# Background scans in a decoder layer: smaller steps, four queues in turn, one operation fewer per chunk state

## The chip, the core and the metric

One Trainium2 chip, one core of it. The metric is the device time of one execution in microseconds (us), lower is better; the number given is the median of the runs shown. Engines: TensorE (PE), VectorE (DVE), ScalarE (ACT), GpSimd (POOL), and SyncE (SP), whose queue starts the transfers.

## What is computed

One inference step of a decoder layer for 1024 prompt tokens and 32 sample tokens (8 sequences of 4) that share the weights, width 1024. Three token mixers run on one input projection: GLA (4 heads, key width 64), FoX attention (4 heads of 128) and HGRN2 (4 heads of 128). Their gated sum goes through `w_out`, then come a SwiGLU block and a last RMSNorm. GLA and HGRN2 are the same gated linear scan:

```
b = cumsum(log_a, within a chunk)
A[t,s] = sum_k q[t,k] k[s,k] exp(b[t,k] - b[s,k])   for s <= t
o = A v + (q exp(b)) S
S = exp(b_last) S + (k exp(b_last - b))^T v
o_a = rms_norm(o_a) * g * silu(gate)
```

The outputs are the activations, the scans' last states for prompt and samples, and FoX's keys, values and forget logs.

## The kernel before

**Layout and products.** All 1056 tokens lie along the free dimension, features on 128 partitions. An fp32 product of full accuracy is made from three fast ones: weight and input are each split into a high and a low part (`split`, L214 and L215), and `gemm` (L115) issues high·high, high·low and low·high per block k of 128 features, in chunks of 352 tokens (L136). A job with 8 blocks has 3 chunks of 24 products; a branch job (4 blocks) 3 chunks of 12.

**Stages.** norm1 and the first jobs (to about 83 us); `in_pairs`, most of the input projection, in which one stage (`pair_run`, L1813) shares sums of operands between pairs of output blocks and FoX's attention runs beside (to 690 us); the mixer stage: 16 jobs for the branch gates and then the first branch jobs, with the scans in the background (690 to 1083 us); a check whether every scan stayed in its safe range (`any_range`, L1437, with a slow path behind a branch that these inputs don't take); the remaining branch jobs, `w_out`, the SwiGLU block and the last norm.

**The background.** Each scan is a Python generator that issues instructions up to its next `yield`. Three queues hold them: `bg3` with two `gla_pair` (L1041), `bg4` with four `hgrn_head` (L1062), and `bgs`, which a `scan` fills with a `scan_sample` (L1340). `gemm` takes one step of `bg3` and of `bgs` after block 3 of every chunk and one of `bg4` and `bgs` at the end of a chunk:

```
if k == 3 and job.kt == KD:
    self.pump(self.bg3, self.bgs)
...
self.pump(self.bg4, self.bgs, *(() if job.kt == KD else (self.bg3,)))
```

At the eighth branch job `second` (L1541) drains what is left.

A scan step is large. `scan` (L1093) makes the cumulated sums (`sums`, L1233), then for each half of 512 tokens `scan_pairs` (DVE subtract and clamp at L1154 and L1155, two exponentials on ACT, two products on POOL at L1158 and L1159), `scan_scores` (matmuls L1172 and L1173, masked copy L1176, transposes L1181), `scan_states` (matmuls L1193; then per chunk ACT L1204, DVE L1205, ACT L1206) and `scan_out` (L1219 and L1221). `scan_sample` prepares its operands (`pair_tile`, L1236 to L1249) one yield before the score matmuls at L1372; then come L1379, L1389, L1394, L1395 and, for the new states, L1413. `head_norm` (L1077, with `rstd` at L229) ends a scan: squares, sums over the partitions, a Newton refinement in three chunks, the gate, and a store to DRAM from where the branch jobs read it. The activations q, k and the decay hold their slots from the first step to the last.

**What sets the order.** The order in which Python issues is a priority only: a scheduler with its own estimates of durations places the instructions on each engine, so a step can stand earlier or later than it was issued. Each engine then works in order.

**ROLL.** In `pair_run` the weights of the next pair are split piece by piece between products, by a table from step to pieces (`ROLL`, L1764); S1 is a DVE subtract (L1753) that needs freshly loaded weights, P1 to P7 are splits.

Of the kernel before, what the change touches and what calls it, by code (L numbers as in the profile page):

```python
# [18 lines left out]
NP = 1024  # L19
# [18 lines left out]
NA, NBU, NH, NAT = 10, 8, 10, 4  # L38
# [52 lines left out]
class Body:  # L91
    def __init__(self, nc, tc, A, O):
        self.nc, self.tc, self.A, self.O = nc, tc, A, O
        self.bg, self.bgs, self.bg3, self.bg4 = [], [], [], []
# [20 lines left out]
    def gemm(self, job, nxt):  # L115
# [13 lines left out]
        for c in range(0 if job.tiles_first else NCW):  # L129
# [3 lines left out]
            for k in range(job.kt):  # L133
# [4 lines left out]
                if k == 3 and job.kt == KD:  # L138
                    self.pump(self.bg3, self.bgs)
# [4 lines left out]
            self.pump(self.bg4, self.bgs, *(() if job.kt == KD else (self.bg3,)))  # L144
# [43 lines left out]
    def pump(self, *qs):  # L188

        if self.cold:  # L190
            return
        for q in qs or (self.bg3, self.bgs, self.bg4):
            if q and next(q[0], "end") == "end":
                q.pop(0)

# [117 lines left out]
    def phase_m(self):  # L313
# [16 lines left out]
        self.bg3 += [self.gla_pair(p) for p in range(2)]  # L330
        self.bg4 += [self.hgrn_head(h) for h in range(4)]
# [323 lines left out]
    def hgrn_gate(self, h, z):  # L655
        nc = self.nc
        l, la = self.u.get(), self.u.get()
# [4 lines left out]
        nc.scalar.activation(z, z, AF.Exp, scale=-1.0, bias=self.log1mlb[:, h:h + 1])  # L662

        nc.vector.tensor_scalar(la, la, self.log1mlb[:, h:h + 1], None, ALU.add)
        nc.scalar.activation(l, la, AF.Abs, bias=self.nloglb[:, h:h + 1])
        nc.scalar.activation(l, l, AF.Exp, scale=-1.0)
        nc.scalar.activation(l, l, AF.Ln, bias=self.one1)
        nc.vector.scalar_tensor_tensor(la, la, self.loglb[:, h:h + 1], l, ALU.max, ALU.add)
        self.u.put(l)
        return z, la  # L670
# [23 lines left out]
    def gla_decay(self, p):  # L694
        nc = self.nc
        z, l = self.u.get(), self.u.get()
        for j in range(4):
# [4 lines left out]
            self.pm.put(ps)  # L702
        self.logsig_part(z, l)
        nc.vector.scalar_tensor_tensor(z, z, 0.0, l, ALU.min, ALU.subtract)
        nc.vector.tensor_scalar(z, z, 1.0 / 16.0, None, ALU.mult)
        self.u.put(l)
        return z
# [333 lines left out]
    def gla_pair(self, p):  # L1041
        yield from self.room(7)
        q, k, *vT = [self.fetch(*t) for t in (("gq", p), ("gk", p), ("gv", 2 * p), ("gv", 2 * p + 1))]
        la = self.gla_decay(p)
        yield
# [9 lines left out]
        yield from self.room(3)  # L1055
        os = [self.u.get(), self.u.get()]
        yield from self.scan(p, q, k, la, vs, vn, os, 64, self.A["sgla"][p], self.O["sgla_p"][p], self.O["sgla_s"][p])
        self.u.put(q, k, la, *vu)
        for i in range(2):
# [1168 lines left out]
```

## Time and profile before

| | us |
|---|---|
| median of the 3 runs | 2011.99 (2006.44 to 2013.47) |
| the profiled execution | 2009.41 |
| its span from the first to the last instruction | 2007.6 |
| PE busy in the span | 1938.9 (97%) |
| DVE busy | 1366.0 (68%) |
| ACT busy | 820.4 (41%) |
| POOL busy | 451.7 (22%) |

The mean granted clock of TensorE over the span is 0.979 of 2.4 GHz. Engines overlap, so the shares don't add up to 100%. Matmuls are pipelined: a row of the timeline gives when the first of a group started and how long the group took, and the next may start before that ends. "L136 <- DVE u" reads: the instruction of line 136 waited for DVE's write to u.

### The profile page before, as it was taken

The numbers are of one execution on the slowest core, as the hardware profiler recorded it, in microseconds if no ns is written. First come the engines' busy times: TensorE is split into PE (matmuls) and PEld (weight loads), VectorE is DVE, ScalarE is ACT, GpSimd is POOL, SyncE is SP. The second block draws the span as 40 slices with busy tenths as digits, with TensorE's granted clock in tenths as the row PEclk, the third lists the DMA queues.
The fourth block names the chain that finished last, engine by engine and source line by source line (L and its number), as shares of the span: only waits on it lengthen the run. The fifth ranks groups of instructions, "written<-read, shape, count | busy, mean of one in ns | idle before, by whom it ended". The sixth has DMA issues, their size and how long they took to land. (4 is left out here: it accounts for less than half of the span.)

```text
span 2007.6 us, 36645 instructions
## 1 busy us (share of the span) xinstructions
PE 1938.9 (97%) x14590; PEld 1821.8 (91%) x14590; DVE 1366.0 (68%) x2267; ACT 820.4 (41%) x1485; POOL 451.7 (22%) x271
## 2 busy tenths in 40 slices
PE   8999999999999999999999999999999999999997
PEld 6889999888988977778899999999999999999997
DVE  8866557544666576866653555878777887668965
ACT  5444444322433354544452343543333333323435
POOL 5211011211222121312100541123222322110004
PEclk9999999999999998979899999999999999999998
DMA  3443432577565533423543443121222122333212
GB/s 142 147 138 121 132 117 85 158 228 228 194 204 187 186 114 115 148 104 141 172 153 115 154 168 118 65 85 64 96 84 77 65 76 76 135 116 121 84 59 87
DMA packets 96982, 253.59 MB, mean 126 GB/s; under 512 B 14562, under 2 KB 28066, under 8 KB 96802
## 3 DMA queue, kind: packets, MB, share of 16 engines
q1 hardware_dynamic: 95250, 249.96, 36.5%
q8 instruction: 117, 1.92, 0.4%
q10 hardware_dynamic: 1296, 0.67, 0.1%
q14 instruction: 63, 0.52, 0.1%
q0 software_dynamic: 256, 0.52, 0.1%
HBM read 183.74 MB, written 67.37 MB: 125 GB/s over the span
## 5 line engine op out<-in xcount | busy, mean ns | idle before, releaser
L136 PE MATMUL pg<-x,wh 128*128 128x352 f32 x1692 | 425.8, 332 | 5.2 <-ACTq L1441 3.2
L1813 PE MATMUL pg<-x,wh 128*128 128x264 f32 x2080 | 401.5, 288 | 7.1 <-POOL frmul L754 2.6
L1813 PEld LDWEIGHTS pg<-x,wh 128*128 128x128 f32 x2080 | 322.8, 188 | 19.9 <-issue 9.6
L136 PEld LDWEIGHTS pg<-x,wh 128*128 128x128 f32 x1692 | 300.6, 192 | 13.3 <-issue 4.3
L1813 PE MATMUL pg<-x,wl 128*128 128x264 f32 x1040 | 295.6, 284 | 0.4 <-DVE wl L215 0.4
L136 PE MATMUL pg<-x,wl 128*128 128x352 f32 x846 | 278.4, 329 | 0.0
L1813 PEld LDWEIGHTS pg<-x,wl 128*128 128x128 f32 x1040 | 195.7, 188 | 0.6 <-DVE wl L215 0.6
L1813 PE MATMUL pg<-x,rh 128*128 128x264 f32 x976 | 187.6, 288 | 2.8 <-DVE fu L1820 2.8
L1813 PE MATMUL pg<-pr,wh 128*128 128x264 f32 x832 | 164.5, 294 | 0.1
L136 PEld LDWEIGHTS pg<-x,wl 128*128 128x128 f32 x846 | 162.7, 192 | 0.0
L1813 PEld LDWEIGHTS pg<-x,rh 128*128 128x128 f32 x976 | 152.2, 189 | 6.3 <-DVE fu L1820 3.2
L215 DVE TENSOR_TENSOR wl<-wf,wh 128x512 fp32r<-128x512 f32 (+2 forms) x125 | 109.7, 880 | 54.0 <-ACT wh L214 43.1
L214 ACT ACTIVATE wh<-wf 128x512 fp32r<-128x512 f32 (+2 forms) x125 | 77.5, 620 | 157.1 <-PE pg L1813 123.9
L1813 PE MATMUL pg<-x,rl 128*128 128x264 f32 x488 | 139.3, 285 | 0.0
L1813 PEld LDWEIGHTS pg<-pr,wh 128*128 128x128 f32 x832 | 130.0, 190 | 9.5 <-issue 5.6
L573 POOL TENSOR_TENSOR pu<-pu,r 128x1056 f32<-128x1056 f32 x21 | 57.3, 2731 | 321.2 <-ACT pu L1822 321.2
L1813 PE MATMUL pg<-pr,wl 128*128 128x264 f32 x416 | 119.0, 286 | 0.0
L1869 POOL TENSOR_TENSOR fu<-fu,r 128x1056 f32<-128x1056 f32 x22 | 67.3, 3059 | 216.9 <-ACT fu L1822 203.7
L107 ACT ACTIVATE wh<-wf 128x1024 fp32r<-128x1024 f32 (+2 forms) x60 | 51.3, 855 | 158.5 <-PE pg L136 143.6
L1820 DVE TENSOR_TENSOR pu<-pu,pg 128x264 f32<-128x264 f32 x132 | 55.8, 426 | 67.0 <-PE pg L1813 66.1
L1822 ACT ACTIVATE pu<-pg 128x264 f32<-128x264 f32 x176 | 66.6, 381 | 67.7 <-PE pg L1813 60.1
L1813 PEld LDWEIGHTS pg<-x,rl 128*128 128x128 f32 x488 | 92.3, 189 | 0.0
(521 smaller groups left out, 4409.6 us busy)
## 6 DMA issues: line engine op xcount, KB each, us to landing
z_dram<-pu SPq DMA_DIRECT2D x44, 528.0 KB
wf<-in_wgu SPq DMA_DIRECT2D x44, 512.0 KB
fa<-in_kc SPq DMA_DIRECT2D x64, 256.0 KB
fa<-in_vc SPq DMA_DIRECT2D x64, 256.0 KB
u<-z_dram SPq DMA_DIRECT2D x30, 528.0 KB
wf<-in_winp SPq DMA_DIRECT2D x30, 512.0 KB
ub<-z_dram SPq DMA_DIRECT2D x22, 528.0 KB
wf<-in_win SPq DMA_DIRECT2D x19, 512.0 KB
```

The costliest lines, as they stand in the source:

```text
L107: nc.scalar.activation(wh[:, :n], wf[:, :n], AF.Copy)
L136: nc.tensor.matmul(ps[:m, :CW], a[:, k, :], b[:, sl], start=n == 0, stop=n == 3 * job.kt - 1)
L214: nc.scalar.activation(h, x, AF.Copy)
L215: (eng or nc.vector).tensor_tensor(l, x, h.bitcast(F32), ALU.subtract)
L573: e[i].tensor_tensor(y[i], y[i], self.r1, ALU.mult)
L1813: nc.tensor.matmul(ps, a[:, w], b, start=first and m == 0, stop=m == 3 * K - 1, skip_group_check=not first)
L1820: nc.vector.tensor_tensor(out, out, ps, ALU.add)
L1822: nc.scalar.activation(out, ps, AF.Copy)
L1869: TT = lambda e, o, x, y, op=ALU.mult: e.tensor_tensor(o, x, y, op)
```

## The change

It has seven parts.

1. `gemm` calls a new `tick` after every block (three products) in place of the two pumps per chunk. `tick` takes one step of one queue; four queues take turns, empty ones are passed over. The fourth, `bgn`, holds the head norms. `hgrn_head(3)` moves from `bg4` to `bg3`.
2. The scans yield more often, and an operation that feeds a matmul is issued one or more yields before it: scores and outputs per head, transposes, states, gates, decay, sample steps, norm steps.
3. Operands are given back early: the samples' columns of q, k and b are copied to small tiles (POOL), so that q, k and the decay go back once both halves are multiplied. Output slots and the norm's gate are fetched late. There are 9 half-size slots instead of 10.
4. States: f2 = f0 of the chunk before times f1 of this one (POOL, once), then T·f2 + U is one DVE operation and T·f2, the scaled state for the outputs, one ACT operation.
5. From DVE to ACT: a bias in the HGRN gate, the 1/16 in the GLA decay, a copy per head in the sample scan.
6. The norm's refinement is done over the whole width instead of three chunks.
7. `ROLL`: S1 one step later, and other pieces moved with it.

```diff
-                if k == 3 and job.kt == KD:
-                    self.pump(self.bg3, self.bgs)
+                self.tick()
...
-            self.pump(self.bg4, self.bgs, *(() if job.kt == KD else (self.bg3,)))
...
+    def tick(self):
+        qs = self.bg3, self.bgs, self.bg4, self.bgn
+        for _ in () if self.cold else qs:
+            q = qs[self.turn % 4]
+            self.turn += 1
+            if q:
+                self.pump(q)
+                return
...
-        self.bg3 += [self.gla_pair(p) for p in range(2)]
-        self.bg4 += [self.hgrn_head(h) for h in range(4)]
+        self.bg3 += [self.gla_pair(0), self.gla_pair(1), self.hgrn_head(3)]
+        self.bg4 += [self.hgrn_head(h) for h in range(3)]
...
+        small = [sp.tile([128, NS], F32, tag="s" + m, name="s" + m, bufs=4) for m in "qkb"]
+        for t, x in zip(small, (q, k, b)):
+            nc.gpsimd.tensor_copy(t, x[:, NP:NT])
...
+        nc.gpsimd.tensor_tensor(f[:, 2, 1:8], f[:, 0, 0:7], f[:, 1, 1:8], ALU.mult)
+        yield
+        self.scan_mul(1, q, k, qe[1], ke[1])
+        self.u.put(q, k, la)
...
+            for h in range(len(vs)):
+                self.scan_scores(At[h], hs[h], qe[hf], ke[hf])
+                yield
...
+            for h in range(len(vs)):
+                self.scan_out(hf, qe[hf], At[h], Sm, vs[h], hs[h], os[h])
+                yield
...
-                nc.scalar.activation(Sm[:, cs], T, AF.Copy, scale=f[:, 0, g - 1:g])
-                nc.vector.scalar_tensor_tensor(Tt[:, cs], Sm[:, cs], f[:, 1, g:g + 1], U[:, cs], ALU.mult, ALU.add)
-                nc.scalar.activation(Sm[:, cs], Sm[:, cs], AF.Copy, scale=f[:, 1, g:g + 1])
+                nc.vector.scalar_tensor_tensor(Tt[:, cs], T, f[:, 2, g:g + 1], U[:, cs], ALU.mult, ALU.add)
+                before.append((Sm[:, cs], T, f[:, 2, g:g + 1]))
...
+        for o, t, g in before:
+            nc.scalar.activation(o, t, AF.Copy, scale=g)
...
+        for m in (2, 1):
+            nc.scalar.activation(E[m], E[m], AF.Exp)
+        nc.scalar.activation(eb, b, AF.Exp)
+        nc.scalar.activation(kh, kh, AF.Exp)
+        yield
...
-    ROLL = {3: (1, "P1", "S1"), 4: (1, "P5", "S2"), 5: (1, "P6", "S3"), 6: (1, "P2", "S4"), 0: (0, "P7"), 1: (0, "P3"), 2: (0, "P4")}
+    ROLL = {3: (1, "P1"), 4: (1, "S1"), 5: (1, "P5", "S2"), 6: (1, "P6", "S3"), 0: (0, "P2", "S4"), 1: (0, "P7", "P3"), 2: (0, "P4")}
```

**How the order moves.** On PE, about 216 products into the mixer stage, before: products (L136; x and wh, wl are the split input and weights), the sample scan's first score matmul (L1372, from skq) between two of them, then a scan half's transposes and scores (L1181, L1172, L1173).

```order
L136 MATMUL pg_96<-x_88,wh_71 128x352
L136 MATMUL pg_96<-x_87,wl_73 128x352
L136 MATMUL pg_96<-x_89,wh_71 128x352
L1372 MATMUL pg_97<-skq 32x32
L136 MATMUL pg_96<-x_90,wh_71 128x352
L1181 MATMUL pg_94<-c_ident,h_8127 128x128 x4
L136 MATMUL pg_96<-x_89,wl_73 128x352
L1172 MATMUL pg_93<-h_8126,h_8127 64x128
L1173 MATMUL pg_93<-h_8126,h_8127 64x64
L1172 MATMUL pg_93<-h_8126,h_8127 64x128
L1173 MATMUL pg_93<-h_8126,h_8127 64x64
```

On PE after, where the same sample scan's scores stand (now L1453; transposes of its keys are L1461, states L1264, prompt outputs L1291 and L1293, products L138):

```order
L138 MATMUL pg_96<-x_79,wh_71 128x352
L138 MATMUL pg_96<-x_80,wh_71 128x352
L138 MATMUL pg_96<-x_79,wl_73 128x352
L1453 MATMUL pg_97<-skq_8423 32x32
L1453 MATMUL pg_98<-skq_8427 32x32
L1453 MATMUL pg_92<-sq,sk 32x32
L1461 MATMUL pg_93<-c_ident,skh 32x128
L138 MATMUL pg_96<-x_81,wh_71 128x352
L138 MATMUL pg_96<-x_82,wh_71 128x352
L138 MATMUL pg_96<-x_81,wl_73 128x352
L1264 MATMUL pg_94<-ub_8145,h_8133 128x128 x4
L138 MATMUL pg_96<-x_83,wh_71 128x352
```

All sample scores of a head stand together, between two sets of three products, and no score of the prompt is beside them.

On PE before, the end of a run of 49 rows without a product: prompt outputs (L1219, L1221), new sample states (L1413), the norm's sums (L229), then products again.

```order
L1219 MATMUL pg_98<-at_8136,ub_8146 128x128
L1221 MATMUL pg_98<-h_8133,h_8132 128x128
L1219 MATMUL pg_98<-at_8136,ub_8146 128x128
L1221 MATMUL pg_98<-h_8133,h_8132 128x128
L1413 MATMUL pg_92<-h_8134,skt 64x512
L1413 MATMUL pg_93<-h_8128,skt 64x512
L1413 MATMUL pg_93<-h_8131,skt 64x512
L229 MATMUL pg_94<-u_8119,ones 128x352
L229 MATMUL pg_97<-u_8119,ones 128x352
L229 MATMUL pg_98<-u_8119,ones 128x352
L136 MATMUL pg_95<-x_85,wh_72 128x352
L136 MATMUL pg_95<-x_86,wh_72 128x352
```

On PE after, prompt outputs of the same stretch and the sample scan's past part (L1471):

```order
L1471 MATMUL pg_94<-u_8121,h_8130 32x128 x8
L138 MATMUL pg_95<-x_77,wh_72 128x352
L138 MATMUL pg_95<-x_78,wh_72 128x352
L138 MATMUL pg_95<-x_77,wl_74 128x352
L1291 MATMUL pg_97<-at_8135,ub_8145 128x128
L1293 MATMUL pg_97<-h_8132,h_8125 128x128
L1291 MATMUL pg_97<-at_8135,ub_8145 128x128
L1293 MATMUL pg_97<-h_8132,h_8125 128x128
L1291 MATMUL pg_97<-at_8135,ub_8145 128x128
L1293 MATMUL pg_97<-h_8132,h_8125 128x128
L1291 MATMUL pg_97<-at_8135,ub_8145 128x128
L1293 MATMUL pg_97<-h_8132,h_8125 128x128
```

Each step now stands between sets of three products. One run without products remains, of 53 rows; it begins 106 rows earlier than the run of 49 did.

On DVE in `in_pairs` before, around S1 (L1753; the ISA rows are FoX's masked maxima):

```order
L215 TENSOR_TENSOR wl_74<-raw_236,wh_72 128x512
L215 TENSOR_TENSOR rl<-wf_69,rh 128x512
L806 ISA fa_821,fs_838<-pg_94,fa_823 128x512
L806 ISA fs_838 128x1
L1753 TENSOR_TENSOR st<-raw_236 128x512
L1757 TENSOR_TENSOR raw_236<-wf_70,raw_236 128x512
```

On DVE after, at the same rows (S1 is L1841):

```order
L223 TENSOR_TENSOR wl_74<-raw_236,wh_72 128x512
L223 TENSOR_TENSOR rl<-wf_69,rh 128x512
L824 ISA fa_818,fs_835<-pg_94,fa_820 128x512
L824 ISA fs_835 128x1
L1841 TENSOR_TENSOR st<-raw_236 128x512
L1845 TENSOR_TENSOR raw_236<-wf_70,raw_236 128x512
```

S1 has kept its neighbours.

## Rows read from the trace of the kernel before

**Rows 1.** The page, part 1, busy time and share of the span, PE

```profile
PE 1938.9 (97%) x14590; PEld 1821.8 (91%) x14590; DVE 1366.0 (68%) x2267; ACT 820.4 (41%) x1485; POOL 451.7 (22%) x271
```

**Rows 2.** Busy time by stretch: length, each engine, PEclk, DMA share, GB/s

```profile
90.00:690.00 600.00, 590.09 (x5089) 538.68 (x5088) 359.04 (x675) 230.71 (x499) 101.14 (x74) 1.00 0.49 161
...
690.00:1083.00 393.00, 376.34 (x2421) 327.74 (x2420) 269.19 (x581) 180.09 (x303) 70.47 (x40) 0.93 0.39 136
...
900.00:970.00 70.00, 70.00 (x454) 63.49 (x453) 50.23 (x97) 33.60 (x51) 17.58 (x8) 1.00 0.42 153
```

**Rows 3.** What PE waited for, 690 to 1083 us: total, times, longest (us)

```profile
PE pg L1372 <- DVE skq L1249: 9.0, 3, 4.7
PE pg L1372 <- DVE at L1176: 2.7, 1, 2.7
PE pg L1429 <- DVE rg_m L1426: 2.1, 1, 2.1
```

**Rows 4.** Timeline of PE at the first long wait: start, us, line

```profile
721.59 0.49 PE L136 MATMUL pg<-x,wh 128*128 128x352 f32 x2
721.91 0.32 PE L136 MATMUL pg<-x,wl 128*128 128x352 f32 x1
722.07 0.32 PE L136 MATMUL pg<-x,wh 128*128 128x352 f32 x1
725.87 0.31 PE L1372 MATMUL pg<-skq 128*32 128x32 f32 x2 [3.48 <-DVE skq L1249]
```

**Rows 5.** Timeline of DVE ahead of the wait that ends at 814.96 us

```profile
813.59 1.23 DVE L1248 TENSOR_TENSOR skq<-sE,u 128x16 f32<-128x16 f32 x1
814.74 0.16 DVE L1249 TENSOR_TENSOR skq<-sE,ub 128x16 f32<-128x16 f32 x1
```

**Rows 6.** Busy time by stretch, the eight stretches with a low clock

```profile
719.00:729.00 10.00, 6.52 (x43) 5.82 (x43) 9.32 (x34) 3.97 (x12) 2.94 (x3) 0.83 0.16 52
766.00:777.00 11.00, 11.00 (x26) 5.50 (x26) 2.44 (x5) 2.12 (x3) 0.00 (x0) 0.53 0.18 72
809.00:822.00 13.00, 8.27 (x58) 6.54 (x56) 12.64 (x37) 2.79 (x9) 2.87 (x3) 0.74 0.27 86
853.00:863.00 10.00, 6.76 (x46) 4.87 (x44) 7.90 (x22) 3.60 (x4) 0.12 (x1) 0.66 0.00 0
871.00:876.00 5.00, 5.00 (x20) 4.25 (x19) 3.26 (x7) 1.71 (x6) 1.80 (x1) 0.66 0.27 110
879.00:890.00 11.00, 11.00 (x63) 8.97 (x63) 2.95 (x5) 5.10 (x7) 0.00 (x0) 0.53 0.23 81
973.00:979.00 6.00, 3.88 (x29) 3.44 (x28) 5.42 (x23) 5.60 (x10) 0.00 (x0) 0.72 0.63 231
984.00:992.00 8.00, 7.63 (x34) 5.28 (x35) 3.96 (x11) 2.55 (x4) 2.68 (x3) 0.57 0.68 210
```

**Rows 7.** Timeline of PE at the beginning of the low clock at 766 us

```profile
765.74 0.49 PE L1219 MATMUL pg<-at,ub 128*128 128x128 f32 x2
...
766.57 0.80 PE L1219 MATMUL pg<-at,ub 128*128 128x128 f32 x2
```

**Rows 8.** Timeline of PE around a group of sixteen small matmuls

```profile
978.29 0.32 PE L136 MATMUL pg<-x,wl 128*128 128x352 f32 x1
978.54 0.65 PE L1389 MATMUL pg<-u,h 128*32 128x128 f32 x16
979.12 0.59 PE L136 MATMUL pg<-x,wh 128*128 128x352 f32 x2
979.55 0.32 PE L136 MATMUL pg<-x,wl 128*128 128x352 f32 x1
```

**Rows 9.** ACT by line, 690 to 1083 us: busy us, mean ns | idle

```profile
L1204 ACT ACTIVATE h<-h,fc 128x128 f32<-128x128 f32 x42 | 16.3, 388 | 6.8 <-DVE h L1201 6.7
...
L1500 ACT ACT_TABLE_LOAD x3 | 3.8, 1283 | 0.1
```

**Rows 10.** What DVE waited for, 90 to 690 us

```profile
DVE st L1753 <- DMA wf<-in_winp: 22.9, 12, 3.8
```

More of the change, by code (lines that the diff above doesn't have):

```diff
@@ L37 @@
 RT128 = float(128.0 ** 0.5)
-NA, NBU, NH, NAT = 10, 8, 10, 4
+NA, NBU, NH, NAT = 10, 8, 9, 4
 KVRING = 3
@@ L1054, in gla_pair @@
             yield
[L1055 to L1059, printed above, removed]
-            yield from self.head_norm(os[i], ("gr", 2 * p + i), self.gng, self.o_dram[2 * p + i])
+        yield from self.scan(p, q, k, la, vs, vn, vu, 64, self.A["sgla"][p], self.O["sgla_p"][p], self.O["sgla_s"][p],
+                             [(("gr", 2 * p + i), self.gng, self.o_dram[2 * p + i]) for i in range(2)])
     def hgrn_head(self, h):
@@ L1070, in hgrn_head @@
         yield
[L1071 to L1077 removed]
+        yield from self.scan(2 + h, q, z, la, [v], [vn], [vu], 128, self.A["shg"][h], self.O["shg_p"][h], self.O["shg_s"][h],
+                             [(("hg", h), self.hng, self.o_dram[8 + h])])
@@ L1078, in head_norm @@
+    def head_norm(self, o, gate, gn, dst, done):
         nc = self.nc
         n = NP if self.cold else NT
-        yield from self.room(5)
-        sq, r, g = self.u.get(), self.u.get(), self.fetch(*gate)
-        nc.scalar.activation(sq[:, :n], o[:, :n], AF.Square)
-        yield
-        yield from self.room(2)
-        yield from self.rstd(r, [sq], 1.0, n)
-        self.u.put(sq)
-        nc.vector.scalar_tensor_tensor(o[:, :n], o[:, :n], gn, r[:, :n], ALU.mult, ALU.mult)
-        nc.gpsimd.tensor_tensor(o[:, :n], o[:, :n], g[:, :n], ALU.mult)
+        while not done:
+            yield
+        yield from self.room(3)
+        slots = v, r, t = [self.u.get() for _ in range(3)]
+        nc.scalar.activation(v[:, :n], o[:, :n], AF.Square)
+        yield
+        yield
+        chunks = [slice(sl.start, min(sl.stop, n)) for sl in self.chunks()]
+        for sl in chunks:
+            w = sl.stop - sl.start
+            ps = self.pm.get()
+            nc.tensor.matmul(ps[:, :w], self.ones, v[:, sl], start=True, stop=True)
+            nc.vector.tensor_scalar(v[:, sl], ps[:, :w], 1.0, EPS, ALU.mult, ALU.add)
+            self.pm.put(ps)
+            yield
+        nc.scalar.activation(t[:, :n], v[:, :n], AF.Ln)
+        nc.scalar.activation(r[:, :n], t[:, :n], AF.Exp, scale=-0.5)
+        yield
+        yield
+        v, t, r1 = v[:, :n], t[:, :n], r[:, :n]
+        nc.vector.scalar_tensor_tensor(t, v, -0.5, r1, ALU.mult, ALU.mult)
+        yield
+        nc.vector.tensor_tensor(t, t, r1, ALU.mult)
+        nc.sync.dma_start(v, self.z_dram[gate][:, :n])
+        yield
+        nc.vector.scalar_tensor_tensor(r1, t, 1.5, r1, ALU.add, ALU.mult)
+        yield
+        nc.vector.scalar_tensor_tensor(o[:, :n], o[:, :n], gn, r1, ALU.mult, ALU.mult)
+        yield
+        nc.gpsimd.tensor_tensor(o[:, :n], o[:, :n], v, ALU.mult)
+        yield
+        yield
@@ L1098, in scan @@
         self.sums(b, 128)
+        yield
         if self.cold:
-            yield
+            yield from self.room(len(vs))
+            os = [self.u.get() for _ in vs]
             S = None
@@ L1105, in scan @@
             self.hf.put(S[1])
+            self.u.put(q, k, la, *vu)
+            for o, x in zip(os, norms):
+                yield from self.head_norm(o, *x, [1])
             return
-        done = []
-        self.bgs.append(self.scan_sample(q, k, b, vn, hs, os, s0_src, sts_out, done))
         sp = self.sp
```

276 lines of the change are left out of this document (153 added, 123 removed).

## Prediction

> **What bounds the kernel now.** I read the page's busy times first, then busy time by stage, then what TensorE waits for in the one stage that the change rewrites, then its clock there, then single operations. The reader is to see in [rows 1] that PE is busy 97% of the span: the kernel is a stream of products, and what can be gained is PE's idle time, the time in which its clock is low, and work on PE that is not needed. The work of the change lies between about 690 and 1083 us, the mixer stage, and by [rows 2] PE is busy there for 376.34 of 393 us, so 16.7 us idle, at a mean granted clock of 0.93. From 90 to 690 us it idles 9.9 of 600 us at a clock of 1.00. So the mixer stage loses 16.7 us by waiting and, at a clock of 0.93, some 27 us by running slowly; all else of the change can only matter if it disturbs PE.
>
> The waits of PE in that stage [rows 3]: 9.0 and 2.7 us in front of L1372, the score products of the sample scan, which wait for small DVE operations (skq of L1249) or for a DVE copy of the prompt's scores (L1176); and 2.1 us for the flag of all_near. The remaining 2.9 us are five smaller places. [Rows 4] show how such a wait looks: products every 0.16 us up to 722.07, then nothing until the L1372 at 725.87. DVE isn't idle meanwhile; 16-column products for the samples stand behind a whole half of the scan's operations in its queue, and one of them took 1.23 us [rows 5]. One generator step issues them and the matmul that needs them, and PE takes its instructions in order.
>
> The clock [rows 6]: eight stretches, 74 us in all, have a granted clock between 0.53 and 0.83, that is, a mixture of 2.4 and 1.2 GHz. Each costs its length times what is missing to 1: 1.7, 5.2, 3.4, 3.4, 1.7, 5.2, 1.7 and 3.4 us, together 25.6 us. The reader should notice two sorts. In five of them (719, 809, 853, 973, 984) PE is busy for less than the whole stretch: a wait stands ahead of the low clock, or in it. In three (766, 871, 879; 12.1 of the 25.6 us) PE is busy 100%, and [rows 7] show the first one begin: the same L1219 pair takes 0.49 us and then 0.80, with no idle time between. What PE did before is a long run of the scans' small matmuls with hardly a product. From 900 to 970 us, where the background comes in small portions, the clock is 1.00 and PE never idles [rows 2]: that is what the change wants of the whole stage.
>
> **The change, part by part.**
>
> *Steps and turns.* By the order of instructions both kernels have 591 background matmuls in the stage's stretch of products; they stand in 64 groups before and 118 after, nearly all of them at a multiple of three products. Runs of more than 20 background matmuls with almost no products between are six before (up to 60) and one after: 63, where GLA pair 0 meets the first heads, since there the planner still gathers what was emitted apart. Everywhere else a run is at most 16. The sample's operands are now issued two or more steps ahead of the matmul, so several groups of products stand between: by four queues in turn, one step comes 6 to 12 products (1 to 2 us at 0.16 us each) after the last one of its queue.
>
> Idle: the two L1372 waits for DVE, 11.7 of 16.7 us, go; 5.0 us I leave (the flag, and small ones). What is late next is DVE in the one long run; I add 2.0 us, about the flag's wait of [rows 3]. So −9.7 us, with ends of −14 and +19 (a wait of the mean size at one in five of the groups; its price is worked out with the first rival).
>
> Clock: falls that follow a wait should go with the wait, falls in a long run with the run. I keep one fall of the larger size (5.2) for the remaining long run and 3.0 for one of the kind that follows a wait: 8.2 of 25.6 us. So −17.4 us; ends −25.6 and 0.
>
> *More switches between kinds of matmul.* More groups mean more passages from 128-row products to matmuls on part of the array and back. [Rows 8] price them: the product at 978.29 starts 0.16 us before its successor could; L1389 starts at 978.54, 0.09 late. The product after it starts at 979.12, and its pair takes 0.43 us to the next start where [rows 4] show 0.32: 0.10 late. So about 0.1 us a passage. By the order there are 149 passages before and 191 after: 42 × 0.1 = +4.2 us. Ends: nothing, where the array drains anyway, and 54 more groups × 0.19 = 10.3 us.
>
> *States.* Per chunk ACT, DVE, ACT becomes one DVE and one ACT operation off the same input. 42 ACT operations of 388 ns [rows 9], 16.3 us, go. ACT is busy 180 of 393 us [rows 2] and no wait of PE worth naming ends on it, so this is worth nothing by itself; it shortens the chain between chunks, which counts in the idle term. If ACT were the cover that ends, it'd cost 16 us the other way, far from its idle 213.
>
> *Moves from DVE to ACT* (a bias, a scaling, a copy per head), *whole-width refinement in head_norm, sample columns copied by POOL, gates loaded late, operand slots given back early*: nothing. DVE is busy 269, POOL 70 of 393 us [rows 2]. The table loads of ACT rise by the order from some 6 to 14 in this stage; 8 × 1.28 us [rows 9] are 10 us on an engine that idles 213, and a late ACT result would show as a wait already counted above. The late gate load is one more thing in SP's queue, behind weight loads; head_norm waits in a queue of its own, and its output is needed only by the last branch jobs. The planner puts the last background matmul at product 1389, and the drain at 1548: 159 products, 26 us, are cover for the last norm's chain. If that cover went, each us of lateness would be paid at the drain.
>
> *ROLL's table.* It is meant to subtract S1 later, when its weights have come; DVE waits 22.9 us for those [rows 10], and all idle time of PE from 90 to 690 us, whoever caused it, is 9.9 us [rows 2]. But by the order S1 stands between the same DVE neighbours as before, and PE's rows are the same up to the mixer. So 0; ends −9.9 (all PE idle gone) and +5 (half as much again).
>
> **The sum** for the profiled execution, 2009.4 us: −9.7 −17.4 +4.2 = −22.9, so 1986.5. The median of the three runs, 2012.0, stands 2.6 above the profiled one, so I expect a median of **1989 us**.
>
> **The rivals.**
>
> 1. *New waits of PE, slower.* A group that comes before its operands stops PE, all products behind it included, and there are now 118 places for it. The mean of today's eleven waits is 16.7 / 11 = 1.5 us. If the clock falls as much as today (most falls begin at a wait), the time is 2009.4 − 16.7 + 4.2 + 1.5 a wait; above today's from 9 waits on, slower by over 0.5% from 15 on. With 30 (one group in four) it is 2042 in the profile, 2045 in the median. For it: steps of one queue return after 1 to 2 us instead of 3.9, and single DVE operations of 1.23 us stand between [rows 5]. Against it: DVE idles a third of the stage, and 900 to 970 us shows steps between products without one wait.
>
> 2. *Idle goes, the clock stays as low as it was.* 2009.4 − 9.7 + 4.2 = 2003.9, 2006 in the median: no change that one can measure. For it: three of eight falls have PE at 100%, and more small groups mean more little gaps at passages. Against it: 900 to 970 us. The Trainium skill, "TensorE: Matmul & The Clock Gate", section "A second HAM failure mode: psum-queue depth-cycling", speaks for this rival: frequent micro-idles between groups of matmuls made the clock swing between its levels in a kernel measured there. That rule would condemn 118 groups more than 64; the trace disagrees with it as far as 900 to 970 us goes, where the clock stays at 1.00.
>
> 3. *Idle goes and the clock comes back but for 3.0 us.* 2009.4 − 9.7 − 22.6 + 4.2 = 1981.3, 1984 in the median: the long run that is left would then not be enough to make it fall. The same page, section "Why this matters for your kernels", advises against idle gaps between bursts as what drops the clock, and by that this would happen as soon as the waits go. The trace agrees for five of the eight stretches and not for 766, 871 and 879 [rows 6], so I don't take it as the likeliest.
>
> 4. *All is won*, waits and falls of the mixer, at no cost of passages, and part of the 9.9 us before it: 2009.4 − 16.7 − 25.6 = 1967, 1970 in the median, down to 1960.
>
> 5. *The change doesn't do what it says*: the planner, which reordered ROLL's step back, gathers the scans' steps in time as it did before. Then 2012. Against it: the order itself, 118 groups.
>
> **How the numbers follow.** The forecast has 0.50, rival 3 0.20, rival 4 0.05: these are faster by over 0.5%, 0.75. Rival 2 with 0.13 and rival 5 with 0.03 are within 0.5% (some 10 us, about what a measurement of this kernel can tell from no change): 0.16. Rival 1 has 0.09. The forecast's own range, with passages from 0 to 10, a clock loss kept between 3 and 15 us and idle kept between 3 and 11, is 1976 to 2006. The range reaches down into rival 4, to 1966, and up past rival 2, to 2010, and leaves out rival 1 and a part of rivals 4 and 5.
>
> **What would show it.** In the profile of the changed kernel PE's idle time between 690 us and the end of the mixer should be about 7 us instead of 16.7, with no wait over 1 us in front of the sample's L1453, the granted clock about 0.98 instead of 0.93, with one fall near the long run of GLA pair 0, and the flag's check should come some 23 us earlier than 1083. S1's waits for its weights (now L1841) should be as they were. It is wrong if waits of PE over 1 us stand at ten or more places (rival 1), if idle time is gone and the clock still at 0.93 (rival 2), or if the gain is found before 690 us.

## The result, and the profile after

| | before | after |
|---|---|---|
| median of the runs, us | 2009.22 (2002.8 to 2013.47) | 1975.60 (1974.96 to 1976.83) |
| profiled execution, us | 2009.41 | 1974.96 |
| its span, us | 2007.6 | 1973.2 |

The ratio is 0.9836 with a 95% interval of 0.9806 to 0.9866: the change makes the kernel 1.6% faster. The forecast was 1989 (1986.5 for the profiled execution) with a range of 1966 to 2010; the time lies in the range, but just below the forecast's own part of it (1976 to 2006), in the piece that was added for rival 4. The gain in the profiled execution is 34.4 us where 22.9 were worked out.

Both kernels do the same 1371 products and 591 background matmuls between the first matmul of the GLA decay (L700, after L713) and the last product ahead of the range check. So this stretch can be taken apart: idle is the length less PE's busy time, lost clock is the length times what the granted clock lacks of 1, and the rest is what remains of the length.

| us | length | idle | lost clock | rest | outside the stretch |
|---|---|---|---|---|---|
| before | 393.0 | 16.7 | 25.6 | 350.7 | 1614.6 |
| after | 361.6 | 8.5 | 3.4 | 349.7 | 1611.6 |
| difference | −31.4 | −8.2 | −22.2 | −1.0 | −3.0 |

The gain is in the mixer stage, as forecast: idle −8.2 (forecast −9.7), clock −22.2 (forecast −17.4), the rest −1.0 (forecast +4.2). Busy time in this stretch after the change answers to the row of 690 to 1083 us in [rows 2]; columns are length, PE, its weight loads, DVE, ACT, POOL, granted clock, DMA share and GB/s.

```profile
690.00:1054.00 364.00, 355.48 (x2434) 313.90 (x2432) 255.56 (x519) 187.86 (x284) 81.00 (x64) 0.99 0.42 148
```

What PE waited for there, which answers to [rows 3]:

```profile
PE pg L138 <- DVE u L1593: 3.1, 1, 3.1
PE pg L1197 <- DVE at L1254: 1.8, 1, 1.8
PE pg L1250 <- POOL h L1241: 1.5, 1, 1.5
PE pg L1197 <- ACT vn L747: 1.3, 1, 1.3
PE pg L138 <- DVE u L648: 0.7, 1, 0.7
```

No wait in front of the sample's scores (L1453) is left; five others are, and the largest is new. The clock has two low stretches instead of eight [rows 6], and both stand right behind a wait; the first and third line show PE idle, the second and fourth the clock behind it:

```profile
706.00:712.00 6.00, 3.24 (x26) 2.69 (x27) 3.72 (x8) 5.96 (x10) 4.88 (x5) 1.00 0.79 261
712.00:718.00 6.00, 6.00 (x51) 5.83 (x48) 5.09 (x11) 5.71 (x11) 2.79 (x4) 0.72 0.41 134
1022.00:1027.00 5.00, 1.91 (x13) 1.62 (x11) 2.92 (x4) 3.92 (x4) 2.44 (x1) 1.00 0.80 276
1027.00:1032.00 5.00, 5.00 (x22) 5.00 (x23) 5.00 (x7) 2.82 (x3) 0.00 (x0) 0.66 0.97 340
```

The long run that is left (53 rows) did not lower the clock, against the forecast, which kept 5.2 us for it:

```profile
721.00:728.00 7.00, 7.00 (x64) 6.11 (x61) 6.91 (x16) 3.71 (x8) 6.17 (x5) 1.00 0.02 5
728.00:738.00 10.00, 10.00 (x99) 8.67 (x98) 7.25 (x21) 5.89 (x15) 0.00 (x0) 1.00 0.15 55
```

S1 still waits for its weights, 25.0 us in 12 waits, as [rows 10] had 22.9 in 12:

```profile
DVE st L1841 <- DMA wf<-in_winp: 25.0, 12, 4.2
```

By the timeline the new wait of 3.1 us hangs on two things that the forecast had put at nothing: table loads on ACT (14 in this stage after 6 before, as forecast) and the norm's refinement over the whole width on DVE. ACT at that place (start, us, instruction):

```profile
1020.10 1.28 ACT L1108 ACT_TABLE_LOAD   x1
1021.40 1.09 ACT L1108 ACTIVATE ub<-u 128x1056 f32<-128x1056 f32 x1
1022.50 1.28 ACT L1109 ACT_TABLE_LOAD   x1
1023.80 1.08 ACT L1109 ACTIVATE ub<-ub 128x1056 f32<-128x1056 f32 x1
```

DVE behind it, with the idle time and its releaser in brackets, and PE behind DVE:

```profile
1024.91 1.55 DVE L1113 SCALAR_TENSOR_TENSOR ub<-u,ub 128x1056 f32<-128x1056 f32 x1 [2.08 <-ACT ub L1109]
1026.39 0.51 DVE L1593 TENSOR_TENSOR u<-pg,u 128x352 f32<-128x352 f32 x1
```

```profile
1026.95 0.61 PE L138 MATMUL pg<-x,wh 128*128 128x352 f32 x2 [3.09 <-DVE u L1593]
```

The norm's logarithm and exponential load a table each, 2.6 us in a row of 4.7; DVE's refinement (L1113) stands in its queue ahead of the eviction of a branch product (L1593), waits 2.1 us for the exponential and takes 1.55 us itself, and the products wait for the bank that the eviction frees. No run left out the loads or the whole width alone, so the shares of the two are not shown.

Of the signs that the prediction names, four came (idle time 8.5 us for about 7, clock 0.99 for about 0.98, no wait in front of L1453, S1's waits as they were) and one did not (a fall near the long run). The end of the stretch comes 32 us earlier, where some 23 were expected for the check.

### The profile page after: what moved, and what is told of

It reads as the page before. It is cut to its first block, busy times and chain, and to the rows that moved or that the text cites. A ratio compares the mean times of both kernels' runs of the same rounds, so it can differ in the third digit from the quotient of the medians.

```text
span 1973.2 us, 36586 instructions
## 1 busy us (share of the span) xinstructions
PE 1914.6 (97%) x14590; PEld 1805.6 (92%) x14590; DVE 1343.3 (68%) x2205; ACT 827.5 (42%) x1465; POOL 464.7 (24%) x295
## 5 line engine op out<-in xcount | busy, mean ns | idle before, releaser
L138 PE MATMUL pg<-x,wh 128*128 128x352 f32 x1692 | 428.8, 335 | 8.9 <-ACTq L1529 3.3
L138 PEld LDWEIGHTS pg<-x,wh 128*128 128x128 f32 x1692 | 295.2, 190 | 31.0 <-issue 14.1
L138 PE MATMUL pg<-x,wl 128*128 128x352 f32 x846 | 276.0, 326 | 0.0
L138 PEld LDWEIGHTS pg<-x,wl 128*128 128x128 f32 x846 | 160.9, 190 | 0.4 <-issue 0.3
```

The lines of the kernel that those rows point to most:

```text
L138: nc.tensor.matmul(ps[:m, :CW], a[:, k, :], b[:, sl], start=n == 0, stop=n == 3 * job.kt - 1)
```

## The experiments

All are timed with their own runs of the kernel before; since that kernel's median moved between 2006 and 2018 us from one set of runs to the next, I compare the experiments' own medians, with the changed kernel's 1975.6 (experiments 1, 3 and 7, from two other sets, lie within 1 us of it). For each the stretch of the profiled execution is taken apart as above.

| us | median (runs) | length | idle | lost clock | rest |
|---|---|---|---|---|---|
| after the change | 1975.6 (1975.0 to 1976.8) | 361.6 | 8.5 | 3.4 | 349.7 |
| 1 old ROLL | 1976.5 (1975.8 to 1983.3) | 362.2 | 11.1 | 0.0 | 351.1 |
| 2 old states | 1988.2 (1986.1 to 1989.1) | 371.0 | 14.0 | 5.1 | 351.9 |
| 3 two turns per 6 | 1975.3 (1974.7 to 1975.9) | 358.9 | 8.1 | 1.7 | 349.1 |
| 4 eight turns per 24 | 1972.6 (1972.0 to 1972.8) | 358.0 | 7.1 | 3.4 | 347.5 |
| 5 before, new states | 2000.5 (1995.7 to 2005.3) | 387.5 | 15.9 | 25.6 | 346.0 |
| 6 before, in turns | 1999.3 (1995.9 to 2005.4) | 383.8 | 14.1 | 18.8 | 350.9 |
| 7 sample not ahead | 1975.2 (1974.0 to 1978.4) | 358.9 | 6.6 | 1.7 | 350.6 |
| 8 slots kept | 1988.6 (1986.8 to 1991.7) | 370.5 | 12.7 | 8.5 | 349.3 |
| 9 before, sample late | 2000.3 (1993.4 to 2009.0) | 385.4 | 19.6 | 18.8 | 347.0 |
| 10 burst | 1998.1 (1992.4 to 2001.1) | 384.3 | 15.0 | 18.8 | 350.5 |
| 11 as 4, two mends | 1988.5 (1987.8 to 1989.1) | 371.7 | 17.3 | 11.9 | 342.4 |
| 12 old states, slots kept | 1992.4 (1990.5 to 1994.3) | 375.4 | 14.9 | 10.2 | 350.3 |

The rest is good to one or two us where the clock hardly falls: experiment 1 has the changed kernel's order on PE and a rest 1.4 us larger. Idle time and lost clock are no closer: the same two profiles differ by 2.6 and 3.4 us, with medians 0.9 us apart. Where much of the stretch is idle at a low clock it is too small, since lost clock then counts idle time twice (experiment 11).

### 1. The old ROLL

```diff
-    ROLL = {3: (1, "P1"), 4: (1, "S1"), 5: (1, "P5", "S2"), 6: (1, "P6", "S3"), 0: (0, "P2", "S4"), 1: (0, "P7", "P3"), 2: (0, "P4")}
+    ROLL = {3: (1, "P1", "S1"), 4: (1, "P5", "S2"), 5: (1, "P6", "S3"), 6: (1, "P2", "S4"), 0: (0, "P7"), 1: (0, "P3"), 2: (0, "P4")}
...
-            self.roll(0, "P6", "S3")
+            self.roll(0, "P6", "S3", "P2", "S4")
```

> The changed kernel with the old ROLL table. By the order PE's rows are the same. If the gain is the scans' steps: 1975.6 us within 2, and DVE's waits for S1's weights near 25 us as before and after. If moving S1 contributed: up to 9.9 us slower (all of PE's idle time from 90 to 690 us), about 1985.

1976.5, the changed kernel's time (one of the four runs took 1983.3). S1's waits for its weights are 23.6 us in 13 waits. ROLL's new table is worth nothing that can be measured, as the order said.

### 2. The old chunk states

```diff
-                nc.vector.scalar_tensor_tensor(Tt[:, cs], T, f[:, 2, g:g + 1], U[:, cs], ALU.mult, ALU.add)
-                before.append((Sm[:, cs], T, f[:, 2, g:g + 1]))
+                nc.scalar.activation(Sm[:, cs], T, AF.Copy, scale=f[:, 0, g - 1:g])
+                nc.vector.scalar_tensor_tensor(Tt[:, cs], Sm[:, cs], f[:, 1, g:g + 1], U[:, cs], ALU.mult, ALU.add)
+                nc.scalar.activation(Sm[:, cs], Sm[:, cs], AF.Copy, scale=f[:, 1, g:g + 1])
```

> The changed kernel with the old chunk states (ACT, DVE, ACT per chunk). If the 42 ACT operations lay beside PE's work, as predicted: 1974 to 1978 us, ACT busy some 16 us more. If the shorter chain from chunk to chunk is what took the waits of PE away: the 8 us of idle time come back, with low clock behind them, 1984 us or more.

12.6 us slower: the prediction's reading falls. ACT's 42 operations more are beside PE's work as far as busy time goes (ACT 199.66 of 374 us), but they lie in a chain, and some outputs now wait for its end. Waits of PE from 690 to 1064 us:

```profile
PE pg L1294 <- ACT h L1278: 3.5, 6, 1.4
PE pg L138 <- DVE u L1594: 3.1, 1, 3.1
PE pg L1197 <- DVE at L1254: 2.4, 1, 2.4
```

L1278 is the last of the three operations of a chunk, L1294 the output product that reads the scaled state. Six such waits are new. With their 3.5 us, and with the scheduler's new order (127 groups), idle time is 5.5 us more, lost clock 1.7, the rest 2.2. What part of the 12.6 us came through the order is not shown.

### 3 and 4. Fewer, larger groups

```diff
-                self.tick()
+                if k % 2 == 1:
+                    for _ in range(2):
+                        self.tick()
```

Experiment 4 has `if k == job.kt - 1: for _ in range(job.kt)` there: all turns of a chunk at its end.

> The changed kernel with two turns behind every six products instead of one behind every three: 93 groups of background matmuls instead of 118, no run longer than 16 but the one of 63. If steps whose operands are issued ahead are enough: 1973 to 1978 us, idle and clock as after the change. If each passage between a product and a background group costs 0.1 us, as the prediction put it, 50 passages fewer are worth 5 us: 1970.5. If products between the steps are what keeps the clock up, 1980 or more.

> The changed kernel with eight turns at the end of each chunk of 24 products: 59 groups, fewer than the 64 before the change, longest runs 36, 28, 27, 26 background matmuls. If the spacing by products is what brought the gain, waits and low clock come back: 1990 to 2005 us, clock in the mixer stage 0.94 or less. If operands issued a step ahead and shorter runs are enough: 1974 to 1982. If a passage costs 0.1 us each, 118 fewer give 12 us: 1964.

1975.3 and 1972.6. The second is 3.0 us faster than the changed kernel, with 59 groups instead of 118 (before: 64). So it is not the spacing by products that brought the gain: here the background stands in lumps of up to 36 matmuls, with the steps and their operands as after the change, and nothing is lost.

```profile
690.00:1051.00 361.00, 353.87 (x2439) 314.87 (x2437) 254.84 (x520) 186.08 (x283) 81.64 (x64) 0.99 0.44 149
```

The passages' price is here too: 59 groups fewer are 118 passages fewer, and the rest is 2.2 us smaller, some 0.02 us a passage where [rows 8] had given 0.1. As the rest is good to one or two us only, this says that a passage costs far less than 0.1 us, and no more than that. This is the version that beats both kernels.

### 5. The kernel before with the new states

```diff
+        nc.gpsimd.tensor_tensor(f[:, 2, 1:8], f[:, 0, 0:7], f[:, 1, 1:8], ALU.mult)
...
-                nc.scalar.activation(Sm[:, cs], T, AF.Copy, scale=f[:, 0, g - 1:g])
-                nc.vector.scalar_tensor_tensor(Tt[:, cs], Sm[:, cs], f[:, 1, g:g + 1], U[:, cs], ALU.mult, ALU.add)
-                nc.scalar.activation(Sm[:, cs], Sm[:, cs], AF.Copy, scale=f[:, 1, g:g + 1])
+                nc.vector.scalar_tensor_tensor(Tt[:, cs], T, f[:, 2, g:g + 1], U[:, cs], ALU.mult, ALU.add)
+                nc.scalar.activation(Sm[:, cs], T, AF.Copy, scale=f[:, 2, g:g + 1])
```

> The kernel before with the new chunk states alone (one DVE and one ACT operation per chunk off the same input). With the old states put back into the changed kernel 12.6 us were lost. If the shorter chain is a gain of its own: some 12 us less than the kernel before, about 2000, from fewer waits and less low clock. If it counts only where steps follow one another closely, or where the long waits for the samples' operands are gone: within 4 us of the kernel before, with the waits in front of L1372-like score products still 9 us or more.

Between the two theories: 0.9963 of the kernel before (0.9937 to 0.9988), some 7 us. The interval goes from 2.4 to 12.7 us, so the run doesn't decide between the two theories, and the edit can be worth as much here as in experiment 2 (12.6). The samples' long waits and the low clock are untouched (25.6 us of lost clock):

```profile
PE pg L1372 <- DVE skq L1249: 9.1, 3, 4.8
```

### 6. The kernel before, taking turns

```diff
-                if k == 3 and job.kt == KD:
-                    self.pump(self.bg3, self.bgs)
+                qs = {1: self.bg3, 3: self.bgs, 5: self.bg4, 7: self.bgs} if job.kt == KD else {1: self.bg4, 2: self.bgs, 3: self.bg3}
+                if k in qs:
+                    self.pump(qs[k])
...
-            self.pump(self.bg4, self.bgs, *(() if job.kt == KD else (self.bg3,)))
```

> The kernel before with its four pumps of a chunk behind four different blocks instead of two and two; steps and operands as they were. By the order 70 groups instead of 64, and the long runs of 60, 45 and 38 background matmuls are still there. If taking turns is what helps: 1990 us or less. If operands issued ahead and small steps are needed: within 8 us of the kernel before, mixer waits 12 us or more and low clock costing 20 us or more.

0.9945 (0.9917 to 0.9972), some 11 us, between the two theories. Turns with the old, large steps bring a third of the gain; the samples' waits are still there:

```profile
PE pg L1372 <- DVE skq L1249: 8.3, 2, 4.8
PE pg L1372 <- DVE at L1176: 3.0, 2, 2.0
```

### 7. The sample's operands in the same step as its scores

Four yields of `scan_sample` go:

```diff
-        yield
         for m in (2, 1):
             nc.scalar.activation(E[m], E[m], AF.Exp)
...
-        yield
         for m in (2, 1):
             ee, oo, qq, kk = [v4(t, m) for t in (E[m], kq[m], q, k)]
...
-        yield
         yield from self.hroom(3)
...
-        yield
         As = [sp.tile([NS, NS], F32, tag=f"As{h}", name="As") for h in range(nh)]
```

> The changed kernel without the yields between the samples' operands and their score products: they're issued in one step again, as before the change. If issuing ahead is what took the waits of 11.7 us away: waits in front of L1453 of 5 to 12 us come back, with low clock of 3 to 10 us behind them, 1984 to 1996 us. If the scheduler or the idle DVE covers them anyway: 1974 to 1979.

1975.2: no wait in front of the scores (now L1449) came back. So the yields that the change adds are not what ended these waits. But the edit doesn't put operands and scores side by side: `hroom(3)`, which yields until three slots are free, is still between them, and on the chip the last operand (now L1437) is done 10 us or more ahead of the first score in all eight groups of scores. The nearest:

```profile
795.59 0.16 DVE L1437 TENSOR_TENSOR skq<-sE,sq 128x16 f32<-128x16 f32 x1
806.26 0.31 PE L1449 MATMUL pg<-skq 64*32 64x32 f32 x4
```

After the change it is 20 us or more. In the kernel before, where two yields stand between the operands and the scores too (L1365 and L1366; not one, as the part on that kernel has it, and not one step, as the prediction and this expectation have it), an operand ends some 0.06 us ahead of the score that waited for it [rows 4, 5]. How far ahead the operands are issued in the program is thus not what tells the two kernels apart; how early DVE gets to them is. What remains of the difference in the program is when a sample scan starts: there as the first thing of a scan, here after both halves of the prompt have their operands. Experiment 9 tries that.

### 8. Slots kept to the end

```diff
-        self.u.put(q, k, la)
         self.near += 1
...
-        self.u.put(*vu)
+        self.u.put(q, k, la, *vu)
```

> The changed kernel with the slots of q, k and the decay given back at the end of a scan, as before the change (the samples still read their small copies). By the order the last background matmul comes at product 1275 of the stage instead of 1176, before the drain. If giving back early is not on the path, as predicted: 1974 to 1979. If later heads start late and their last norm collides with the branch jobs: 1980 or more, with waits behind 1000 us.

13.0 us slower; the prediction had put giving back early at nothing. One way in which a slot makes PE wait is to be seen around 902 us, on POOL, ACT and PE in this order:

```profile
899.02 2.43 POOL L1122 TENSOR_TENSOR u<-u,u 128x1056 f32<-128x1056 f32 x1 [11.08 <-DVE u L1120]
```

```profile
901.48 1.08 ACT L1097 ACTIVATE u<-ub 128x1056 f32<-128x1056 f32 x1 [7.64 <-POOL u L1122]
902.47 1.26 ACT L1281 ACTIVATE h<-h,fc 128x128 f32<-128x128 f32 x4
```

```profile
902.91 0.49 PE L1292 MATMUL pg<-h,h 128*128 128x128 f32 x2 [2.61 <-ACT h L1281]
```

A norm's square (L1097) gets the slot that another norm's gate product on POOL still reads. ACT waits 7.6 us for it, the scaled states stand behind it in ACT's queue, and the outputs wait 2.6 us for them. The longest wait of this run is another one:

```profile
PE pg L158 <- DVE u L648: 3.1, 1, 3.1
```

```profile
980.36 0.95 PE L158 MATMUL pg<-x,wh 128*128 128x352 f32 x2 [3.09 <-DVE u L648]
```

There products need a bank whose eviction (L648) stands in DVE's queue behind the operations of a scan and of the samples that now come later; the clock is low behind it. The last background matmul moves from product 1176 of the stretch to 1275. From the check to the end this profile has 921.3 us instead of 915.9, but experiment 12, whose background ends as late, has 917.6, so most of that is not the slots' doing.

### 9. The kernel before, samples two steps later

```diff
-NA, NBU, NH, NAT = 10, 8, 10, 4
+NA, NBU, NH, NAT = 10, 8, 11, 4
...
-        self.bgs.append(self.scan_sample(q, k, b, vn, hs, os, s0_src, sts_out, done))
...
         ab1 = self.scan_pairs(1, q, k, b)
         yield
+        self.bgs.append(self.scan_sample(q, k, b, vn, hs, os, s0_src, sts_out, done))
```

> The kernel before, with one thing moved: a scan puts its sample scan into the queue two steps later, when its operands for both halves of the prompt are made (as the changed kernel does), with 11 half-size slots instead of 10, which that needs. By the order the first sample score then stands 50 rows later on PE. If the waits of 11.7 us came from the samples' small DVE operations standing behind the prompt's: they go, and with them the low clock behind them (some 13 of 25.6 us): 1985 to 1995 us. If they come from operands issued in the same step as the product: they stay, 2000 us or more.

The waits of L1372 are gone, all of them, though operands and scores are issued as before; the last operand now ends 2.7 us or more ahead of the first score. Other waits stand in their place, so that idle time is 19.6 us instead of 16.7, and the time is a miss:

```profile
PE pg L1181 <- POOL h L1158: 4.4, 2, 4.2
PE pg L1429 <- DVE rg_m L1426: 4.4, 1, 4.4
PE pg L1172 <- POOL h L1159: 3.5, 4, 1.7
```

So the 11.7 us came from the place of the samples' operations in front of the prompt's (the eleventh slot was not tried alone), but what the forecast subtracted for them is not to be had by that alone: the next late thing, the prompt's own operands from POOL, then shows. The time is 0.9955 of the kernel before (0.9926 to 0.9984).

### 10. One burst

```diff
                 self.pump(q)
-                return
+                break
+        self.ticks += 1
+        if self.ticks == 160:
+            for _ in range(30):
+                self.pump(*qs)
```

> The changed kernel, but at the 160th turn thirty steps of each queue are issued at once. By the order two runs of 72 and 93 background matmuls then stand close together, with 19 products between. If a long run with few products lowers the clock by itself: a fall to 1.2 GHz near them in a stretch where PE is 100% busy, 5 us or more lost there, 1980 us or more. If the clock falls only after waits: 1.00 wherever PE is busy, and any fall stands behind a wait.

22.5 us slower, with a long low clock. Busy time by stretch:

```profile
800.00:806.00 6.00, 3.27 (x26) 1.80 (x26) 4.36 (x14) 5.02 (x7) 0.21 (x1) 0.77 0.14 55
806.00:826.00 20.00, 20.00 (x76) 13.36 (x77) 10.31 (x28) 3.64 (x10) 0.41 (x2) 0.50 0.15 54
```

The clock is 1.00 from 800 to 803 us and 0.50 from 803.2 us on. That is behind a wait of 0.5 us and ahead of one of 2.3 us, and the new sample states (L1505) run just then:

```profile
800.00:803.00 3.00, 2.52 (x24) 1.76 (x24) 2.62 (x9) 2.11 (x2) 0.00 (x0) 1.00 0.27 111
803.20:806.00 2.80, 0.55 (x3) 0.04 (x2) 1.73 (x5) 2.71 (x5) 0.20 (x1) 0.50 0.00 0
```

```profile
802.40 1.31 PE L1505 MATMUL pg<-h,skt 32*128 32x512 f32 x2 [0.48 <-DVE at L1258]
805.96 1.34 PE L1268 MATMUL pg<-ub,h 128*64 128x128 f32 x10 [2.25 <-ACT h L1202]
```

It stayed at 1.2 GHz for 20 us in which PE was 100% busy with background matmuls. After the change, where products follow a wait, the two low stretches cost 1.7 us each; these 20 us cost 10. So the fall was long in this burst; the run doesn't tell whether the matmuls or the waits began it, as both stand there.

### 11. Two mends

On top of experiment 4, DVE instead of POOL copies the samples' columns, and three more turns stand between the norm's exponential and the DVE operation that reads it:

```diff
-            nc.gpsimd.tensor_copy(t, x[:, NP:NT])
+            nc.vector.tensor_copy(t, x[:, NP:NT])
...
         nc.scalar.activation(r[:, :n], t[:, :n], AF.Exp, scale=-0.5)
+        yield
+        yield
+        yield
         yield
         yield
```

> Eight turns at the end of each 24 products (1972.6 us in its own run), and two mends: the samples' columns copied by DVE instead of POOL, where a copy of 1.24 us stood ahead of the first scan's product, and three more turns between the norm's exponential and the DVE operation that waits for it. If those two waits (1.5 and up to 3.1 us, with low clock behind) go: 1967 to 1971 us. If DVE becomes late with the copies, or the last norm collides with the drain: 1973 to 1978.

A miss, 1988.5. The wait of the first scan for POOL stays (2.2 us in 2 waits), and the later norms collide with the branch jobs: one wait of 11.5 us, up to 1052 us. Ahead of the eviction DVE refines a norm, late because it waited for the exponential until 1037 us (L1118), splits the last heads' outputs (L225) and begins the next norm.

```profile
PE pg L138 <- DVE u L1598: 11.5, 1, 11.5
PE pg L1255 <- POOL h L1246: 2.2, 2, 1.6
```

```profile
1037.22 1.26 DVE L1118 SCALAR_TENSOR_TENSOR u<-ub,u 128x1056 f32<-128x1056 f32 x1 [3.70 <-ACT u L1111]
1043.86 4.64 DVE L225 TENSOR_TENSOR x<-ub,x 128x1056 fp32r<-128x1056 f32 x2
```

This run also has a fall with no wait ahead of it, in a stretch of outputs and new states without a product (L1296, L1298, L1506 from 815.4 us):

```profile
812.00:820.00 8.00, 8.00 (x45) 6.40 (x43) 6.07 (x18) 4.88 (x12) 3.13 (x3) 1.00 0.36 122
820.00:828.00 8.00, 8.00 (x29) 7.19 (x29) 0.00 (x0) 1.07 (x2) 2.38 (x2) 0.57 0.54 201
```

### 12. Old states and slots kept together

The edits of 2 and 8.

> The changed kernel with two parts undone together: q, k and the decay given back at the end of a scan, and the old chunk states. Alone they lost 13.0 and 12.6 us. If each takes away a delay of its own they add: about 2001 us. If both are one and the same reserve (a scan's later steps come late, PE waits), the second costs little once the first is gone: 1989 to 1994. If they multiply (late heads meet slow chains): 2008 or more, the kernel before.

1992.4, 16.8 us slower than the changed kernel; apart they lost 12.6 and 13.0, so 8.8 of 25.6 us are shared, as the second theory has it. Waits of PE from 690 to 1068 us:

```profile
PE pg L1293 <- ACT h L1277: 4.4, 3, 3.4
PE pg L158 <- DVE u L648: 3.0, 1, 3.0
```

Both long waits are those of experiment 8: the one behind the norm's slot has grown from 2.6 to 3.4 us, and the six short ones of experiment 2 are no longer there as such. That both parts count by how late the scaled states come to the outputs fits this wait; for the whole of the 16.8 us it is not shown.

## Why the prediction was right, and where not

**Place and sign.** Right: the mixer stage gained 31.4 of 34.4 us, by less idle time and a higher clock, and by the clock more than by the waits. Of the rivals, the third (the clock comes back but for 3.0 us) came nearest in its mechanism: 3.4 us are left, at 1984 forecast and 1975.6 measured. In time rival 4 (1970) is nearer, which also has no cost of passages.

**How much of it was luck.** The forecast put the whole gain on steps and turns and nothing on states and slots. Without these two parts the kernel takes 1992.4 us (12), which is nearer to the 1989 than the 1975.6 are. One of the three terms of the sum is right in size, two are too cautious by some 5 us each, and two parts put at nothing are worth 16.8 us together; that the time still lies in the range is in part luck.

**Idle, forecast −9.7, measured −8.2.** The size was right and the reason wrong. "One generator step issues them and the matmul that needs them" misreads the kernel before, which has two yields there, and the added yields are not why the samples' waits went (7). In the kernel before it is enough to start a sample scan later in its scan, and they go (9): DVE then has the operands ready in time. Experiment 9 also shows that other waits come up once these are gone; which parts of the change keep them away was not tried. Of the 8.5 us left, 4.6 are new (3.1 for DVE, 1.5 for POOL).

**Clock, forecast −17.4, measured −22.2.** The term was mis-sized by the 5.2 us kept for the long run. That run of 53 rows is at 1.00 throughout, while [rows 6, 7] show a fall in one of 49. A count of rows was the wrong measure; the runs that fell without a wait, at 766 us before and at 820 us in experiment 11, are of outputs and new states of the samples, the one of 53 rows has scores, transposes and states between its outputs. The traces kept have nine falls in this stage that begin with PE busy all the while (766, 872 and 879 us before, three in experiment 5, two in 6, one in 11), and each has new sample states just ahead of it. These alone don't do it, though: after the change the same states run, and no fall is without a wait. Whether the kind of matmul is the difference was not tried.

**Passages, forecast +4.2, measured in the rest −1.0.** Mis-sized: one group's edges in [rows 8] stood for all, at 0.1 us a passage; experiment 4 gives about 0.02. Also, steps of one kind now stand together: by the order the changes from one kind of background matmul to another fell from some 100 to some 30, which the prediction did not count. That this is why the rest did not grow is not shown: in experiment 4 some 80 are there by its trace, and the rest is smaller still.

**States, forecast nothing, experiment 12.6.** The step that failed is "no wait of PE worth naming ends on it, so this is worth nothing by itself". In the changed kernel six waits of PE end on the old chain (2). The prediction read the waits of the kernel before, where such waits come to 0.2 us. There the same edit is worth some 7 us (5), not nothing either; that the chain was hidden there behind the samples' waits and large steps would explain a difference to 12.6, but the interval of (5) reaches that far, so it is not shown. A chain has to be read against the waits that are left after the change.

**Operands given back early, forecast nothing, experiment 13.0.** The step that failed weighed busy times (DVE 269, POOL 70 of 393 us) and not who waits for a slot and what then comes late. Experiment 8 shows it on ACT, 7.6 us for a slot with the scaled states queued behind (2.6 us of PE), and on DVE, where the later scan's operations hold up an eviction (3.1 us of PE).

**Table loads and the refinement over the whole width, forecast nothing.** Partly wrong: 2.6 us of loads in a row on ACT held DVE, and through DVE's queue, with the 1.55 us of the refinement itself, PE for 3.1 us, with a low clock behind (5 us at 0.66). Moves from DVE to ACT and the late gate loads were not undone.

**ROLL, forecast nothing.** Right (1).

**The premise** that small portions between products are what the stage needs was wrong as a reason: lumps of eight turns are as good and 3.0 us better (4). The Trainium skill, "TensorE: Matmul & The Clock Gate", section "A second HAM failure mode: psum-queue depth-cycling", on which rival 2 drew, would have frequent small gaps between groups make the clock swing. More groups alone don't do it here: 118 groups and 59 groups both have 0.99, and the kernel before with 64 had 0.93. As PE idles 8.5 us in all after the change, there are hardly any gaps between the groups, and what frequent ones would do no run here shows. The Trainium skill's advice on the same page, in "Why this matters for your kernels", against idle gaps between bursts agrees with the low stretch at 1027 us after the change, behind a wait of 3.1 us, and as far as waits go with the one at 712, behind two shorter ones (1.3 and 1.5 us); it does not agree with the fall at 820 us in experiment 11, which has none.

**What stays open.** Undoing states and slots together gives back 16.8 of 33.6 us. Where the other half lies is not shown: the smaller steps, the later samples, the norms' own queue, the moves to ACT and the rest of the change were not undone one by one. In the kernel before, turns (6) and later samples (9) gave 0.55% and 0.45% alone, and it was not tried whether they add. What sets off a fall of the clock, a wait or a run of outputs and new states, is not settled either.

## What to carry to other kernels

An edit that no wait of today asks for can still be worth something once the change has taken today's waits away: before costing it at nothing, look at what would be late next, and test it by undoing that part alone. Issuing an operand earlier in the program doesn't make it early on the chip: look at when its engine gets to it, and what stands ahead of it in that engine's queue. In an in-order machine the price of a busy slot or of a chain is paid by what is queued behind the waiting instruction, on another engine; total busy time of that engine doesn't tell it. A wait on TensorE costs more than its length where the clock falls behind it, so the first thing to look at after the waits is the granted clock right behind them.

## What the runs showed that was not expected

The kernel before doesn't have one time: the 19 runs of it beside experiment 10 lie between 1997.05 us (mean granted clock 0.987) and 2018.64 us (0.972), and the shorter ones are those with the higher clock. The four of the changed kernel lie within 1.9 us, at 0.990 to 0.992. So the change seems to make the time steadier as well as shorter, with four runs to show it; experiment 1, with the same order on PE, has one run of four at 1983.3.
